# The S5 part in another order, skip and router sums on GpSimd, expert weights in 4 MB pieces

## Chip, cores and metric

The kernel runs on one core of one Trainium2 chip. The metric is the device time of one execution in microseconds (us). A profiled execution comes with it: its span goes from the first to the last instruction, its time also covers what lies around them. Engines are TensorE (PE; weight loads are PEld), VectorE (DVE), ScalarE (ACT), GpSimd (POOL) and SyncE (SP), which issues nearly all transfers.

## What is computed

One layer of a decoder on 256 tokens of width 1024: an S5 state-space mixer (48 groups of 16 channels, 64 complex states each) beside a cross-attention into 256 memory tokens, one output projection, layer norm, a mixture of 32 experts (four for each token), layer norm. All numbers are float32.

```python
p = x @ w_in                                   # 768 columns for S5, 256 for attention
y_mix = s5_mixer(p[:, :768], ...)              # scan over time, + d_skip * u, gelu, y * sigmoid(y @ w_glu + b_glu)
y_mem = attention(p[:, 768:], mem @ w_k, mem @ w_v)       # 4 heads of 64
h = layer_norm(ALPHA * x + concat(y_mix, y_mem) @ w_out, ln1_g, ln1_b)
logits = h @ router_w + router_b               # top 4 of 32, softmax over the four
for e in range(32):                            # only the tokens that chose e
    gu = h @ w_gu[e] + b_gu[e]                 # 1024 -> 2048
    g, l = min(gu[:, :1024], 7), clip(gu[:, 1024:], -7, 7)
    y += gate[e] * ((g * sigmoid(1.702 * g) * (l + 1)) @ w_down[e] + b_down[e])
out = layer_norm(ALPHA * h + y, ln2_g, ln2_b)
```

## The kernel before

**Memory.** One SBUF tile `big` holds 23 slots of 1 MB (128 partitions x 8 KB). `slot_of` gives every named matrix a slot, several names share one in turn. Two neighbouring slots make a block of 2 MB; 11 blocks form `ring`, in the order in which the front part lets go of them. `next_block` turns the ring by one block.

**Order.** Every instruction on TensorE, ScalarE, VectorE and SP is chained to the one before it in the program (`pin`), so each of these engines runs in the order of the text. GpSimd is not chained. A transfer on SP waits until the last reader of its block is done, and all transfers behind it wait too.

**Front part.** S5 runs in 32 chunks of 8 steps. The group matrices `m1p` (state input, three tiles of 16 groups) and `m2` (state output, three tiles) are made by `power` on VectorE, sums partly on GpSimd. `kb` (from line 578) makes the kernels within a chunk, with the skip `dsk` added by a TensorE product with the identity, and ScalarE copies them to `kr`. Then, in the order of the text: first half of K (`kps`), turning of biases and norms (`bgp`, to `gcol` and `bglu`), router bias (`rbp`: `ln1_b @ router_w` on TensorE, 8 products, and one for `router_b`), turning of `kr` (`kc`), copies of it to other rows (`shifted(0)`), second half of K, scores, row maxima, chunk powers (`doubled(NC)`), `shifted(1)`, turning of `m1p` (`m1_turned`, banks `m1tp`), chunk inputs `s_in` (banks `sip`), turning of these (banks `stp`, to `sv`), exponentials, V projection (`vmp`), `shifted(2)`, `rotated` twice (the scan over chunks), reciprocals and products for the softmax, products within the chunk (`yb`, called Yt), attention output (`pTp`, `pv`), `xs` on VectorE, products with the chunk states (`yb`, called Yx), out-projection of the attention, gelu, gate (`zp`), `wsp` (column sums of `router_w * ln1_g`, summed over k by VectorE as `wgs`, then over partitions by TensorE), the rest of the out-projection (`yp`), norm and router.

**Experts.** For each expert SP loads `w_gu` in four pieces of 2 MB, `load_gu` (two k-tiles each; every partition gets 16 KB that lie together in memory), and `w_down` in two. Per expert TensorE does: `up` (banks `gu`, 64 products seen in the trace), for every second expert `gather_pair` (tokens of two experts picked from `h_sb`) or else `combine` (adding two experts' results into `accp`, which the first call also sets up), `act_t` (turning of the activations), `up_bias`, `down`. At the end expert 31's `up` comes ahead of expert 30's `down`; all that uses the banks `tail`. Expert 31's `act_t` stands behind expert 30's `down` and ahead of its own.

Of the kernel before, what the change touches and what calls it, by code (L numbers as in the profile page):

```python
# [28 lines left out]
ROWS = 2  # L29
NBIG = 23  # L30
# [11 lines left out]
def kernel(  # L42
# [47 lines left out]
    )):  # L90
        for name in names.split():
            slot_of[name] = k
# [5 lines left out]

    ring = [2 * k + n for k in (0, 1, 2, 3, 4, 8, 6, 10, 7, 9, 5) for n in range(0, 2, ROWS)]

# [478 lines left out]
    for b in range(3):  # L579
# [41 lines left out]
    dbg("@KM", None)  # L621

    proj("kps", kT, lambda q, kt: wk[:, kt, P * q : P * q + P], lambda q, kt: memT[:, kt, :], (0,))
# [7 lines left out]
    wg, wgs, lfix = keep_t("wg", (P, KT, NE)), small("wgs", (P, NE)), keep_t("lfix", (P, 2, NE))  # L631
# [7 lines left out]
    tv = [t.rearrange("p (g t h) -> p g t h", t=Q, h=NH) for t in tz]  # L639
    for b in range(3):  # L640
        for a in range(2):
            ps = bank(f"kc{b}{a}")
            for l in range(4):
                tr(ps[:, P * l : P * l + P], kr[:, 4 * b + l, NH - NH * a : NH - NH * a + P])
            S.copy(tv[b][:, :, Q - 1 - a, :], ps.rearrange("p (g h) -> p g h", h=2 * NH)[:, :, 0:NH])

    def shifted(b):
        for m, rows in ((1, ((32, 64), (64, 96), (96, 128))), (2, ((64, 128),)), (3, ((96, 128),))):
            for r0, r1 in rows:
                S.copy(  # L650
                    tv[b][r0:r1, :, Q - 2 - 2 * m : Q - 2 * m, :],
                    tv[b][r0 - 32 * m : r1 - 32 * m, :, Q - 2 : Q, :],
                )

    tj = [tz[(g % 12) // 4][:, P * (4 * (g % 4) + g // 12) :][:, 0:P] for g in range(NG)]

    shifted(0)
    dbg("@KM1", None)
    proj("kps", kT, lambda q, kt: wk[:, kt, P * q : P * q + P], lambda q, kt: memT[:, kt, :], (1,))
    dbg("@LG1", None)  # L660
    wgl += load_wgl(1)
    dbg("@SM", None)
    scores = []
    for i in range(2):
        sc = [bank(f"sc{i}{e}") for e in range(2)]
        for h2 in range(2):
            for e in range(2):
                pe = slice(64 * e, 64 * e + 64)
                mm(
                    sc[e][:, NT * h2 : NT * h2 + NT], xqT[pe, h2, i * P : (i + 1) * P], kT[pe, h2, :],  # L670
                    True, True, True,
                )
        scores.append(sc)

    dbg("@SMb", None)
    prob = big_tile("prob").rearrange("p (i h m) -> p i h m", i=2, h=4)
    sums = []
    for i, sc in enumerate(scores):
        mx, sm = small(f"mx{i}", (P, 4)), small(f"sm{i}", (P, 4))
        for e in range(2):  # L680
            V.tensor_reduce(
                out=mx.rearrange("p (h e) -> p e h", e=2)[:, e, :],
                in_=sc[e].rearrange("p (h m) -> p h m", h=2), axis=AX.X, op=ALU.max,
            )
        ts(mx, mx, -0.125, ALU.mult)
        sums.append((mx, sm))
    doubled(NC)
    shifted(1)
# [44 lines left out]
    for i, sc in enumerate(scores):  # L733
        mx, sm = sums[i]
        for hd in range(4):
            S.activation(
                prob[:, i, hd, :], sc[hd % 2][:, NT * (hd // 2) : NT * (hd // 2) + NT], AF.Exp,
                bias=mx[:, hd : hd + 1], scale=0.125, accum_out=sm[:, hd : hd + 1],
            )
    dbg("@VM", None)  # L740
    proj("vmp", vm, lambda q, kt: memT[:, kt, P * q : P * q + P], lambda q, kt: wv[:, kt, :], (0,))
    shifted(2)
    dbg("@VM1", None)
    proj("vmp", vm, lambda q, kt: memT[:, kt, P * q : P * q + P], lambda q, kt: wv[:, kt, :], (1,))

    dbg("@SC1", None)
# [7 lines left out]
    def rotated(o, x0, x1, op):  # L754
# [3 lines left out]
        V.tensor_tensor_scan(out=o, data0=r8f, data1=ta, initial=0.0, op0=ALU.mult, op1=ALU.add)  # L758

    rotated(g_re, s_re, s_im, ALU.add)  # L760
    dbg("@SMr", None)
    for i, (_, sm) in enumerate(sums):
        V.reciprocal(sm, sm)
        for hd in range(4):
# [693 lines left out]
```

## Time and profile before

| | us |
|---|---|
| median of three runs | 1074.6 (1073.11 to 1078.62) |
| the profiled execution, its time | 1072.42 |
| its span | 1070.6 |
| TensorE busy | 1003.3 (94% of the span) |
| VectorE / ScalarE / GpSimd busy | 245.6 / 150.4 / 49.2 |

The DMA engines read 421.9 MB from HBM, 402.7 MB of it expert weights. The page's chain of work that ended last gives 50% of the span to TensorE and 45% to DMA. Matmuls are pipelined and their ends are modelled, so a busy TensorE isn't one at its peak.

### The profile page before, as it was taken

How to read it: one execution, taken by the hardware profiler on the slowest of the kernel's cores; microseconds unless marked ns; L12 is line 12 of the kernel's file. 1: busy time of each engine (PE TensorE's matmuls, PEld its weight loads, DVE VectorE, ACT ScalarE, POOL GpSimd, SP SyncE). 2: the span in 40 equal slices, each digit the busy share in tenths (PEclk: the TensorE clock that was granted, in tenths of full speed). 3: DMA queues.
4: the chain of work that ended last, by engine and by line, in shares of the span. 5: the costliest groups of instructions: out<-in, count | busy, mean ns of one | idle time of the engine just before them, and what ended most of it. 6: DMA issues, size and time to landing. Idle time of an engine off the chain costs nothing.

```text
span 1070.6 us, 12357 instructions
## 1 busy us (share of the span) xinstructions
PE 1003.3 (94%) x5297; PEld 442.6 (41%) x5297; DVE 245.6 (23%) x531; ACT 150.4 (14%) x288; POOL 49.2 (5%) x90
## 2 busy tenths in 40 slices
PE   9999999999999999999999988899999999898994
PEld 8886554434343434343434332323333343333331
DVE  7984251111111111111111111110111111111113
ACT  3494020101010101010101000000101110100001
POOL 5810000000000000000000000000000000000001
PEclk9999999999999999999999999999999999999998
DMA  9949989999999999999999999999999999999992
GB/s 303 166 151 329 424 314 429 428 417 430 427 428 427 425 429 428 426 430 427 428 426 429 429 409 428 429 428 427 427 427 428 427 428 427 427 428 428 429 422 98
DMA packets 43939, 424.61 MB, mean 397 GB/s; under 512 B 11251, under 2 KB 14215, under 8 KB 19177
## 3 DMA queue, kind: packets, MB, share of 16 engines
q1 hardware_dynamic: 43384, 422.73, 95.9%
q10 hardware_dynamic: 496, 1.05, 0.3%
q8 instruction: 43, 0.70, 0.3%
q14 instruction: 16, 0.12, 0.0%
HBM read 421.93 MB, written 1.84 MB: 396 GB/s over the span
## 4 chain that ended last, share of the span: by engine, by line
PE 50%; DMA 45%; DVE 2%; ACT 1%; issue 0%; SPq 0%; ACTq 0%; POOL 0%; DVEq 0%; POOLq 0%
DMA big<-in_exp_w_gu_dram 29%; PE gu_e L142 20%; PE dn_e L142 11%; DMA big<-in_exp_w_down_dram 11%; PE xgp_e L142 4%; DMA big<-in_exp_b_down_dram 4%; PE accp L142 3%; PE yp L142 3%; DVE big L135 2%; PE ups L142 1%; PE zp L142 1%; DMA big<-in_l_w_in_dram 1%; PE tail L142 1%; ACT big L135 1%; PE atp_e L145 1%; PE qps L142 1%
## 5 line engine op out<-in xcount | busy, mean ns | idle before, releaser
L142 PE MATMUL gu_e<-big,xg_e 128*64 128x512 f32 x1984 | 439.8, 594 | 44.2 <-DMA big<-in_exp_w_gu_dram 43.5
L142 PEld LDWEIGHTS gu_e<-big,xg_e 128*64 128x64 f32 x1984 | 138.3, 137 | 340.0 <-issue 253.0
L142 PE MATMUL dn_e<-big,xl_te 128*64 128x512 f32 x960 | 212.6, 595 | 0.0
L142 PEld LDWEIGHTS dn_e<-big,xl_te 128*64 128x64 f32 x960 | 66.3, 137 | 144.3 <-issue 119.6
L1127 DVE TENSOR_SCALAR xl_e<-gu_e 128x512 f32<-128x512 f32 x31 | 21.4, 691 | 429.2 <-PE gu_e L142 429.2
L1155 DVE COPY y_e<-dn_e 64x512 f32<-64x512 f32 x30 | 20.5, 684 | 265.7 <-PE dn_e L142 265.7
L135 ACT ACTIVATE gu_e<-xl_e 128x512 f32<-128x512 f32 x31 | 18.6, 601 | 403.7 <-DVE xl_e L1127 403.7
L142 PEld LDWEIGHTS xgp_e<-oh_e,big 128*128 128x128 f32 x544 | 65.4, 196 | 13.3 <-PE gu_e L142 12.2
L142 PE MATMUL xgp_e<-oh_e,big 128*128 128x128 f32 (+1 forms) x544 | 68.7, 284 | 0.0
L142 PE MATMUL accp<-y_e,ogT_e 128*128 128x512 f32 x128 | 59.4, 603 | 0.8 <-DVE y_e L1155 0.8
L135 ACT COPY y_e<-dn_e 64x512 f32<-64x512 f32 x30 | 17.5, 582 | 244.0 <-DVE y_e L1155 244.0
L142 PEld LDWEIGHTS accp<-y_e,ogT_e 128*128 128x128 f32 x128 | 23.2, 190 | 35.3 <-issue 33.7
L142 PE MATMUL gu_e<-bgu,ident 32*64 32x512 f32 x248 | 34.3, 612 | 0.0
L135 DVE TENSOR_TENSOR big<-big 128x96 f32<-128x96 f32 (+8 forms) x47 | 29.0, 635 | 21.1 <-ACT big L135 16.2
L142 PE MATMUL yp<-big 128*128 128x512 f32 x64 | 28.6, 596 | 0.0
L135 DVE TENSOR_TENSOR big<-big,tab 128x2048 f32<-128x2048 f32 x12 | 26.5, 2276 | 0.2 <-DVE big L135 0.2
L135 ACT COPY xl_te<-atp_e 128x512 f32<-128x512 f32 x30 | 17.9, 595 | 60.4 <-PE atp_e L145 57.5
L135 ACT COPY xg_e<-xgp_e 128x512 f32<-128x512 f32 x32 | 18.8, 587 | 53.4 <-PE xgp_e L142 53.4
L1131 DVE TENSOR_TENSOR xr_e<-xr_e,gu_e 128x512 f32<-128x512 f32 x31 | 21.3, 687 | 6.4 <-ACT gu_e L135 3.3
L135 POOL TENSOR_TENSOR yv<-yv,mhalf 128x1 f32<-128x1 f32 x2 | 1.1, 550 | 468.9 <-DVE yv L135 468.9
L1238 POOL MEMSET big<- 128x1280 f32 (+1 forms) x2 | 2.1, 1058 | 447.0 <-PE gu_e L142 447.0
L1130 DVE SCALAR_TENSOR_TENSOR xr_e<-xr_e,xl_e 128x512 f32<-128x512 f32 x32 | 22.1, 692 | 1.1
(289 smaller groups left out, 586.7 us busy)
## 6 DMA issues: line engine op xcount, KB each, us to landing
big<-in_exp_w_gu_dram SPq DMA_DIRECT2D x128, 2048.0 KB, 39.1
big<-in_exp_w_down_dram SPq DMA_DIRECT2D x62, 2048.0 KB, 33.8
big<-in_l_w_in_dram SPq DMA_DIRECT2D x3, 1024.0 KB
big<-in_w_out_dram SPq DMA_DIRECT2D x3, 1024.0 KB, 9.2
big<-in_exp_w_down_dram SPq DMA_DIRECT2D x3, 1024.0 KB
big<-in_x_dram SPq DMA_DIRECT2D x3, 512.0 KB, 3.5
big<-in_l_s_w_glu_dram SPq DMA_DIRECT2D x2, 768.0 KB
big<-in_l_w_in_dram SPq DMA_DIRECT2D x2, 512.0 KB, 6.8
```

What stands on the lines that cost most here:

```text
L135: return lambda *a, **k: pin(f(*a, **k))
L142: pin(PE.matmul(o, lhsT, rhs, start=start, stop=stop, skip_group_check=shared))
L145: pin(PE.transpose(o, in_, ident if idn is None else idn))
L1127: V.tensor_scalar(out=xl_, in0=ps[0], scalar1=7.0, scalar2=None, op0=ALU.min)
L1130: V.scalar_tensor_tensor(out=xr, in0=xr, scalar=1.0, in1=xl_, op0=ALU.add, op1=ALU.mult)
L1131: a = V.tensor_tensor(out=xr, in0=xr, in1=sg, op=ALU.mult)
L1155: eng(y[:, 512 * dh : 512 * dh + 512], ps[dh][64 * dh : 64 * dh + 64, :])
L1238: G.memset(t[:, 0:width], 0.0)
```

## The change

- In the text, `m1_turned` (three tiles), `s_in` and `sv` move up to right behind `bgp`, ahead of `kc`. The first half of K moves behind `kc`. `shifted(1)`, `doubled(NC)` and the first `rotated` come ahead of the row maxima, as does the first half of V with `shifted(2)`; the second `rotated` comes ahead of the reciprocals.
- The skip is added by GpSimd to `kr` instead of by TensorE in the bank. For the router bias GpSimd multiplies `router_w * ln1_b`, VectorE sums it over k, and `wsp` sums both over partitions and adds `router_b`; `rbp` is gone.
- Slots are renumbered so that the ring is 0, 2, 4 to 20 and blocks that follow each other in it mostly lie side by side; `s_in` shares another slot.
- `w_gu` is cut in groups of four k-tiles (a partition has 32 KB that lie together). For experts 3 to 28, where the two blocks are neighbours, one transfer of 4 MB takes both; otherwise two of 2 MB. The gather follows the new numbering.
- Expert 31's `act_t` comes between the two halves of expert 30's `down`.

```diff
@@ ring and slots
+    free_order = (0, 1, 2, 3, 4, 8, 6, 10, 7, 9, 5)
-        "ptmp0 wsc", "ptmp1 gt", "m20", "m21", "m22", "u_sb", "cab s_in tw yg", "memT xs", "bbt tz0", "bab att",
-        "mem_sb tz1 gb", "ut kr pT x2", "x_sb m1p1 wgl2", "xT prob", "rawb m1p2 wo0", "rawc m1p0 wo1", "win_2 wo3",
+        "ptmp0 wsc", "ptmp1 gt", "m20", "m21", "m22", "u_sb", "cab tw yg", "memT xs", "bbt tz0", "bab att",
+        "mem_sb tz1 gb", "ut kr pT x2", "x_sb m1p1 wgl2", "xT s_in prob", "rawb m1p2 wo0", "rawc m1p0 wo1", "win_2 wo3",
-            slot_of[name] = k
+            slot_of[name] = 2 * free_order.index(k // 2) + k % 2 if k < 22 else k
-    ring = [2 * k + n for k in (0, 1, 2, 3, 4, 8, 6, 10, 7, 9, 5) for n in range(0, 2, ROWS)]
+    ring = list(range(0, 22, ROWS))
@@ kb
-        mm(pv_[:, :, 0:NH], ident, dsk[:, 4 * b : 4 * b + 4, :], False, True, True)
         S.copy(kr[:, 4 * b : 4 * b + 4, NH:144], pv_)
+    tt(kr[:, :, NH : 2 * NH], kr[:, :, NH : 2 * NH], dsk, ALU.add, G)
@@ behind doubled(16)
-    proj("kps", kT, lambda q, kt: wk[:, kt, P * q : P * q + P], lambda q, kt: memT[:, kt, :], (0,))
...
     S.copy(bglu, bgp[:, 0:6])
-    rbp = bank("rbp")
-    for kt in range(KT):
-        mm(rbp[:, 0:NE], gcol[:, KT + kt : KT + kt + 1].to_broadcast([P, P]), wr[:, kt, :], kt == 0, False)
-    mm(rbp[:, 0:NE], ones[0:1, :], rb, False, True)
-    S.copy(lfix[:, 1], rbp[:, 0:NE])
+    def m1_turned(j):
...
+    m1t = m1_turned(0)
+    m1t += m1_turned(1)
+    m1t += m1_turned(2)
+    s_in = big_tile("s_in")[:, 0:1536].rearrange("p (l n) -> p l n", l=6)
...
@@ behind kc
+    proj("kps", kT, lambda q, kt: wk[:, kt, P * q : P * q + P], lambda q, kt: memT[:, kt, :], (0,))
     shifted(0)
@@ behind the scores
+    shifted(1)
+    doubled(NC)
...
+    rotated(g_re, s_re, s_im, ALU.add)
+    proj("vmp", vm, lambda q, kt: memT[:, kt, P * q : P * q + P], lambda q, kt: wv[:, kt, :], (0,))
+    shifted(2)
@@ behind the second half of V
-    rotated(g_re, s_re, s_im, ALU.add)
+    rotated(g_im, s_im, s_re, ALU.subtract)
     for i, (_, sm) in enumerate(sums):
         V.reciprocal(sm, sm)
...
-    rotated(g_im, s_im, s_re, ALU.subtract)
@@ router
-    tt(wg, wr, gcol[:, 0:KT].unsqueeze(2).to_broadcast([P, KT, NE]), ALU.mult, G)
+    for q, w_ in enumerate((wg, wb)):
+        tt(w_, wr, gcol[:, KT * q : KT * q + KT].unsqueeze(2).to_broadcast([P, KT, NE]), ALU.mult, G)
...
-    V.tensor_reduce(out=wgs, in_=wg.rearrange("p k e -> p e k"), axis=AX.X, op=ALU.add)
+    for q, w_ in enumerate((wg, wb)):
+        V.tensor_reduce(out=wgs[:, q], in_=w_.rearrange("p k e -> p e k"), axis=AX.X, op=ALU.add)
...
-    mm(wsp[:, 0:NE], ones, wgs, True, True)
+    mm(wsp[:, 0 : 2 * NE], ones, wgs.rearrange("p q e -> p (q e)"), True, False)
+    mm(wsp[:, NE : 2 * NE], ones[0:1, :], rb, False, True)
     S.mul(lfix[:, 0], wsp[:, 0:NE], -1.0)
+    S.copy(lfix[:, 1], wsp[:, NE : 2 * NE])
@@ gather
-    hv = h_sb.rearrange("p i (t r j) -> p i t j r", r=P, j=ROWS)
+    hv = h_sb.rearrange("p i (t r j) -> p i t j r", r=P, j=GJ)
@@ down
+            if kk == KT // 2:
+                between()
@@ load_gu
+        for t in range(KT // GJ):
+            rows = src[t * GJ * P : (t + 1) * GJ * P, :].rearrange("(p j) n -> p j n", j=GJ)
+            next_block(), next_block()
+            k0, k1 = ring[-2:]
+            if whole and k1 == k0 + ROWS:
+                b = big[:, 2048 * k0 : 2048 * (k0 + GJ)].rearrange("p (j n) -> p j n", j=GJ)
+                SP.dma_start(b, rows)
+                w += [b[:, j, :] for j in range(GJ)]
+                continue
+            for n, k in enumerate((k0, k1)):
+                b = big[:, 2048 * k : 2048 * (k + ROWS)].rearrange("p (j n) -> p j n", j=ROWS)
+                SP.dma_start(b, rows[:, ROWS * n : ROWS * n + ROWS])
+                w += [b[:, j, :] for j in range(ROWS)]
@@ the experts' loop
+        gu = load_gu(w_gu[0, e], 3 <= e < NE - 3) if e < NE - 1 else gu_last
...
-            down(f"e{e}", at, lambda kk: dn[kk], y[0:64, :], [tb[0]] * 2)
+            last_at = []
+            down(
+                f"e{e}", at, lambda kk: dn[kk], y[0:64, :], [tb[0]] * 2,
+                lambda: last_at.append(act_t(f"e{e + 1}", a, tb[3])),
+            )
...
-            at = act_t(f"e{e}", a, tb[3])
-            down(f"e{e}", at, lambda kk: dn[kk], y[64:P, :], tb[1:3])
+            down(f"e{e}", last_at[0], lambda kk: dn[kk], y[64:P, :], tb[1:3])
```

## Rows read from the trace of the kernel before

**Rows 1.** The page: slices of transfer rate (26.8 us each); a DMA issue line.

```profile
GB/s 303 166 151 329 424 314 429 428 417 430 427 428 427 425 429 428 426 430 427 428 426 429 429 409 428 429 428 427 427 427 428 427 428 427 427 428 428 429 422 98
...
big<-in_exp_w_gu_dram SPq DMA_DIRECT2D x128, 2048.0 KB, 39.1
```

**Rows 2.** Windows: us, then busy us (instructions) by engine, PEclk, DMA share, GB/s.

```profile
134.00:140.00 6.00, 6.00 (x33) 4.04 (x32) 4.62 (x13) 0.59 (x1) 0.00 (x0) 1.00 0.24 55
...
240.00:1040.00 800.00, 755.16 (x3662) 290.67 (x3660) 120.81 (x252) 71.30 (x132) 2.05 (x2) 1.00 1.01 427
```

**Rows 3.** Timeline, TensorE at the end: start us, us, engine, line, instruction [idle before].

```profile
1042.06 3.65 PE L142 MATMUL tail<-big 128*64 128x512 f32 x16 [1.14 <-DMA big<-in_exp_w_down_dram]
...
1045.64 0.75 PE L145 MATMUL tail<-ident,xr_e 128*128 128x128 f32 x4
...
1047.72 7.09 PE L142 MATMUL tail<-big,xl_te 128*64 128x512 f32 x32 [1.33 <-ACT xl_te L135]
```

**Rows 4.** Timeline of VectorE in the front part.

```profile
62.20 1.27 DVE L135 TENSOR_REDUCE mx<-sc 128x2 f32<-128x512 f32 x2
...
64.98 1.95 DVE L135 TENSOR_TENSOR big<-big,e__413 128x384 f32<-128x384 f32 x4
...
72.02 2.88 DVE L135 TENSOR_TENSOR big<-big 128x768 f32<-128x768 f32 x3 [4.15 <-PE stp L145]
74.93 1.76 DVE L135 TENSOR_TENSOR_SCAN big<-big 128x768 f32<-128x768 f32 x1
...
81.37 7.48 DVE L135 TENSOR_TENSOR big<-big 128x744 f32<-128x744 f32 x8
```

**Rows 5.** Timeline of ScalarE in the front part.

```profile
55.90 3.13 ACT L135 COPY big<-big 32x512 f32<-32x512 f32 x5
...
62.61 5.97 ACT L135 COPY big<-m1tp 128x512 f32<-128x512 f32 x12
...
71.09 1.83 ACT L135 COPY big<-stp 128x512 f32<-128x512 f32 x4
...
76.41 0.43 ACT L135 COPY big<-vmp 128x256 f32<-128x256 f32 x1
```

**Rows 6.** Timeline of TensorE in the front part.

```profile
43.16 0.43 PE L142 MATMUL kb<-dsk,ident 128*128 128x64 f32 x2
...
46.19 3.67 PE L142 MATMUL kps<-big 128*128 128x256 f32 x16
...
52.63 2.84 PE L145 MATMUL kc<-ident,big 128*128 128x128 f32 x24
...
58.86 2.19 PE L142 MATMUL sc<-big 64*128 64x256 f32 x16
...
72.07 7.07 PE L142 MATMUL vmp<-big 128*128 128x256 f32 x32
```

**Rows 7.** A window of 2 us behind the stream.

```profile
1050.00:1052.00 2.00, 2.00 (x12) 0.64 (x10) 0.00 (x0) 0.00 (x0) 0.00 (x0) 1.00 0.08 33
```

**Rows 8.** Timeline of SP's queue: single issues of expert 4's blocks.

```profile
216.63 0.33 SPq L135 DMA_DIRECT2D big<-in_exp_w_gu_dram  x1
...
232.98 0.33 SPq L135 DMA_DIRECT2D big<-in_exp_w_gu_dram  x1
```

**Rows 9.** A window of 1 us after that issue.

```profile
234.00:235.00 1.00, 1.00 (x8) 0.37 (x6) 0.00 (x0) 0.00 (x0) 0.00 (x0) 1.00 1.16 328
```

**Rows 10.** DMA packets from 300 to 360, 1044 to 1052 and 16 to 20 us.

```profile
DMA packets 1763, 25.65 MB, mean 427 GB/s; under 512 B 197, under 2 KB 197, under 8 KB 197
...
q1 hardware_dynamic: 1760, 25.61, 100.4%
...
DMA packets 314, 1.48 MB, mean 185 GB/s; under 512 B 43, under 2 KB 43, under 8 KB 223
...
q1 hardware_dynamic: 314, 1.48, 45.0%
...
q1 hardware_dynamic: 375, 1.46, 98.0%
```

More of the change, by code (lines that the diff above doesn't have):

```diff
@@ L29 @@
 ROWS = 2
+GJ = 4
 NBIG = 23
@@ L630 @@
     S.copy(bglu, bgp[:, 0:6])
-    wg, wgs, lfix = keep_t("wg", (P, KT, NE)), small("wgs", (P, NE)), keep_t("lfix", (P, 2, NE))
-    rbp = bank("rbp")
-    for kt in range(KT):
-        mm(rbp[:, 0:NE], gcol[:, KT + kt : KT + kt + 1].to_broadcast([P, P]), wr[:, kt, :], kt == 0, False)
-    mm(rbp[:, 0:NE], ones[0:1, :], rb, False, True)
-    S.copy(lfix[:, 1], rbp[:, 0:NE])
[L639 to L687, printed above, removed]
@@ L688 @@
-    shifted(1)
+    wg, wb = keep_t("wg", (P, KT, NE)), small("wb", (P, KT, NE))
+    wgs, lfix = small("wgs", (P, 2, NE)), keep_t("lfix", (P, 2, NE))
     dbg("@M1B", None)
@@ L731, with shifted @@
             S.copy(dst[:, l0:l1], ps[:, 0 : P * (l1 - l0)].rearrange("p (l j c) -> p l j c", j=4, c=NC))
[L733 to L744, printed above, removed]
+    tv = [t.rearrange("p (g t h) -> p g t h", t=Q, h=NH) for t in tz]
+    for b in range(3):
+        for a in range(2):
+            ps = bank(f"kc{b}{a}")
+            for l in range(4):
+                tr(ps[:, P * l : P * l + P], kr[:, 4 * b + l, NH - NH * a : NH - NH * a + P])
+            S.copy(tv[b][:, :, Q - 1 - a, :], ps.rearrange("p (g h) -> p g h", h=2 * NH)[:, :, 0:NH])
+    def shifted(b):
+        for m, rows in ((1, ((32, 64), (64, 96), (96, 128))), (2, ((64, 128),)), (3, ((96, 128),))):
+            for r0, r1 in rows:
+                S.copy(
+                    tv[b][r0:r1, :, Q - 2 - 2 * m : Q - 2 * m, :],
+                    tv[b][r0 - 32 * m : r1 - 32 * m, :, Q - 2 : Q, :],
+                )
+    tj = [tz[(g % 12) // 4][:, P * (4 * (g % 4) + g // 12) :][:, 0:P] for g in range(NG)]
+    dbg("@KM", None)
+    proj("kps", kT, lambda q, kt: wk[:, kt, P * q : P * q + P], lambda q, kt: memT[:, kt, :], (0,))
+    shifted(0)
+    dbg("@KM1", None)
+    proj("kps", kT, lambda q, kt: wk[:, kt, P * q : P * q + P], lambda q, kt: memT[:, kt, :], (1,))
+    dbg("@LG1", None)
+    wgl += load_wgl(1)
+    dbg("@SM", None)
+    scores = []
+    for i in range(2):
+        sc = [bank(f"sc{i}{e}") for e in range(2)]
+        for h2 in range(2):
+            for e in range(2):
+                pe = slice(64 * e, 64 * e + 64)
+                mm(
+                    sc[e][:, NT * h2 : NT * h2 + NT], xqT[pe, h2, i * P : (i + 1) * P], kT[pe, h2, :],
+                    True, True, True,
+                )
+        scores.append(sc)
+    shifted(1)
+    doubled(NC)
     dbg("@SC1", None)
@@ L760 @@
     rotated(g_re, s_re, s_im, ALU.add)
+    dbg("@VM", None)
+    proj("vmp", vm, lambda q, kt: memT[:, kt, P * q : P * q + P], lambda q, kt: wv[:, kt, :], (0,))
+    shifted(2)
+    dbg("@SMb", None)
+    prob = big_tile("prob").rearrange("p (i h m) -> p i h m", i=2, h=4)
+    sums = []
+    for i, sc in enumerate(scores):
+        mx, sm = small(f"mx{i}", (P, 4)), small(f"sm{i}", (P, 4))
+        for e in range(2):
+            V.tensor_reduce(
+                out=mx.rearrange("p (h e) -> p e h", e=2)[:, e, :],
+                in_=sc[e].rearrange("p (h m) -> p h m", h=2), axis=AX.X, op=ALU.max,
+            )
+        ts(mx, mx, -0.125, ALU.mult)
+        sums.append((mx, sm))
+    for i, sc in enumerate(scores):
+        mx, sm = sums[i]
+        for hd in range(4):
+            S.activation(
+                prob[:, i, hd, :], sc[hd % 2][:, NT * (hd // 2) : NT * (hd // 2) + NT], AF.Exp,
+                bias=mx[:, hd : hd + 1], scale=0.125, accum_out=sm[:, hd : hd + 1],
+            )
+    dbg("@VM1", None)
+    proj("vmp", vm, lambda q, kt: memT[:, kt, P * q : P * q + P], lambda q, kt: wv[:, kt, :], (1,))
+    rotated(g_im, s_im, s_re, ALU.subtract)
     dbg("@SMr", None)
@@ L1143, in act_t, with down @@
         return at
-    def down(n, at, w_of, y, ps=None):
+    def down(n, at, w_of, y, ps=None, between=lambda: None):
         ps = [bank(f"dn_{n}")] * 2 if ps is None else ps
         for kk in range(KT):
+            if kk == KT // 2:
+                between()
             w = w_of(kk)
@@ L1181, in combine_on, with load_gu @@
                 tt(acc[:, i, ds_], acc[:, i, ds_], ps, ALU.add)
-    def load_gu(src):
+    def load_gu(src, whole=False):
         w = []
-        for t in range(KT // ROWS):
-            b = next_block().rearrange("p (j n) -> p j n", j=ROWS)
-            SP.dma_start(b, src[t * ROWS * P : (t + 1) * ROWS * P, :].rearrange("(p j) n -> p j n", j=ROWS))
-            w += [b[:, j, :] for j in range(ROWS)]
+        for t in range(KT // GJ):
[11 more added lines that the diff above has]
+                w += [b[:, j, :] for j in range(ROWS)]
         return w
```

7 lines of the change are left out of this document (3 added, 4 removed).

## The prediction

> **What bounds the kernel now.** Read first the page's slices of transfer rate [rows 1]: from the sixth slice on (each is 26.8 us) the core's DMA engines move about 428 GB/s to the end, while the six slices before that are uneven. The windows [rows 2] say the same sharply: 427 GB/s at a share of 1.01 from 240 to 1040 us, and 55 GB/s from 134 to 140. So all sixteen engines work without a pause from 140 us on, and the weights of 32 experts (32 x 12.58 MB) pass through them in order. Eight of the ring's 2 MB blocks come free and are loaded before 134 us; the rest, some 386 MB, starts when the output projection lets go of the next blocks at about 140 us, and 386 MB at 427.5 GB/s is 903 us, which gives 1043 us. The trace has TensorE taking up the last block but those of the last expert at 1042.06 [rows 3]. Three things therefore set the time: when the front part hands over (140 us), how long the stream runs (903 us), and what comes behind it (28.5 us up to 1070.6). In the stream TensorE first works off its lead of eight blocks and then waits for weights; time saved on it there is worth nothing. The times below go by the profiled execution, 1072.4 us with a span of 1070.6; the median of the three runs is 1074.6, 2.2 above it, and I add that at the end.
>
> **The front part.** Up to 89 us VectorE, ScalarE and TensorE hand each other work. In the trace of before VectorE idles 4.15 us ahead of the first rotation, waiting for the turned chunk states `stp` [rows 4], since ScalarE copies the twelve banks of `m1tp` only from 62.6 to 68.6 [rows 5]. The change puts this block ahead of `kc`, the K projection and the scores. I follow the new chain with the old durations.
> TensorE leaves `kb` at 46.2 [rows 6]; the three products with `dsk` (0.43 each) are gone, so at 45.0. ScalarE has copied `kb`, `gcol` and `bglu` at about 46, then the twelve `m1tp` copies take 5.97: 52.0. From there to the last `stp` copy it was 4.3 us before (68.6 to 72.9) [rows 5]: 56.3. VectorE is in its own queue until 62.2, then `doubled(NC)` takes 3.0 and the first rotation 4.8 [rows 4]: 70.0. So the old wait is gone, and what is late next is the other branch. TensorE: `kc` after `stp`, 2.84, until 58.7; first K projection 3.67 until 62.4. ScalarE copies it (0.43 for such a copy of `vmp` [rows 5]) and then, behind it in its queue, runs `shifted(0)` (3.13) until 65.9; the second projection is done at 66.1 and copied at 66.5; of the scores (2.19) the last three quarters need both halves of K: 68.1. V projection, first half of 7.07: 71.6; copy and `shifted(2)` on ScalarE: 75.1; the eight exponentials, which lay between `stp` and the copy of `vmp`, take 3.6 [rows 5]: 78.7. VectorE has been done with the row maxima (2.8) at 72.8 and with the second rotation (4.6) at 77.4, but now **the reciprocals stand ahead of the products for `xs` in its queue** and wait for the exponentials: `xs` starts at 79.0 and takes 7.48 [rows 4], so it ends at 86.5, and the Yx products on TensorE start there instead of at 88.85. That is 2.4 us. Behind it TensorE is busy without a break up to the end of the output projection, and one product is added ahead of the latter: the router bias joins `wsp`, and a small product of two instructions lasts about 0.4, as those with `dsk` do [rows 6], some 0.3 of it on the path. GpSimd's two router products and VectorE's second sum over them lie beside TensorE's products with `w_glu`; with that cover gone the second sum, of 256 elements a row, would cost less than a product of 768 does, 0.96 (2.88 for three [rows 4]). So the hand-over comes **2.1 us earlier**. The best case is VectorE never waiting: 62.2 + 3.0 + 4.8 + 2.8 + 4.6 + 7.5 = 84.9, 4.0 earlier. The worst is nothing: GpSimd makes the `kr` sum, which no row shows, and if it is queued behind the second `m2` sum, TensorE and all that follows may start some 2 us later.
> All SP issues of this part keep their order; the copy of `x2` waits for `pv` as before, and the idle stretch at 134 to 140 us swallows small delays of the eight blocks ahead of it.
>
> **The tail.** Before, TensorE turned the last expert's activations after the last product of expert 30: products of the second half from 1042.06, turning at 1045.64, ScalarE's copy behind another copy, and the last expert's products only at 1047.72 [rows 3]. Now the turning stands between the two halves, where TensorE waits 1.14 us for weights anyway (four turnings, 0.75), and the copy is hidden behind the second half. The last products start at 1045.64: **2.1 us** less. They need their weights: the engines are nearly done at 1050 (share 0.08 from there to 1052 [rows 7]), and the last two k-tiles are wanted at 1051 and 1051.9, so they just arrive in time; were they late, 1.1 us would be lost. Bounds: 1.0 to 2.1 saved.
>
> **The 4 MB pieces, cost.** A whole piece takes two neighbouring blocks of the ring, so SP waits for the later one. Over most of the stream there is enough in flight (39 us from issue to landing in the median [rows 1]) for that to cost nothing. Early on there isn't. For expert 4 SP issued its third 2 MB block at 216.63 and the fourth at 232.98 [rows 8], since no block comes free while TensorE builds `accp` and then starts expert 2's second product. Around 234 to 235 the rate falls to 328 GB/s [rows 9]: the queue was just running dry when the fourth arrived. After the change the third is tied to the fourth and goes out at 233 with it. The queue is then 2 MB poorer when it counts: 2.1 MB at 427.5 GB/s is **4.9 us** of idle engines, and since the stream is the bound it is never made up. Behind SP's wait stand only loads whose blocks come free later still. The same happens once before, at expert 3, whose third block is tied to a fourth that comes free later, but whatever idles there shortens the later queue no further: together one block. Further on what is in flight grows from expert to expert, up to the 39 us [rows 1], and no gap as long as this 16 us comes again, since `accp` is set up only once: I count no other dry spot. Bounds: 3.9 (the engines that lag were not dry yet) to 5.7.
>
> **The 4 MB pieces, gain.** Each partition's run grows from 16 to 32 KB, half as many packets. In a window of nothing but expert weights [rows 10] 1566 data packets of 16 KB take 100.4% of 16 x 60 us: 614 ns each. Near the end 91 packets of 8 KB and 180 of 4 KB (1.48 MB) take 45.0% of 16 x 8 us, 57 us. With a constant c per packet and one rate both hold for c = 9 ns. Per 4 MB piece each engine saves eight constants and one small closing packet, which I price at the constant too: 9 x 9 = 81 ns. By the ring (11 blocks, 10 from expert 18 on) 44 pairs of experts 3 to 28 are neighbours, 41 of them behind the dry spot: 41 x 81 ns = **3.3 us** saved. Bounds: 0, if 32 KB still moves as two packets of 16, since the trace has none above 16; and 8.5, by the early window of 4 KB packets [rows 10], where 98.0% of 64 us over 375 packets is 167 ns for 3.9 KB, so c = 23 ns. I take 9, from the same kind of load.
> The Trainium skill speaks of both ends. Its page "DMA: Bandwidth & Descriptors", section "Rules for kernel authors", asks for 128 partitions and at least 1 MiB per DMA for full bandwidth; the 2 MB pieces satisfy that, so by it the gain would be 0. The same page, "Why small descriptors are slow (HBM only)", names about three fixed cycles per packet; at the 850 MHz that it gives for the fabric that is by my estimate 3.5 ns, less than the 9 ns of the rows, and the gain would be 1.3 us. The rows decide for 9 ns.
>
> **Other edits.** The gather reads `h_sb` with a stride of four elements instead of two; the turning of activations reads with a stride of four already, and TensorE has slack in the stream: nothing. The renumbered ring keeps its order: nothing.
>
> **Sum.** 1072.4 - 2.1 - 2.1 + 4.9 - 3.3 = 1069.8; on the scale of the median, **1072.0**.
>
> **The rivals.** (a) 32 KB moves as two packets of 16: the gain falls away, 1072.0 + 3.3 = 1075.3. For it: no packet above 16 KB in the trace. Chance 0.20. (b) The dry spot does not cost: the queue holds more than I read, or the lagging engines ride through it, 1072.0 - 4.9 = 1067.1. Against it: the 328 GB/s at 234. Chance 0.20. (c) A packet costs 23 ns beyond its bytes, 1072.0 - 5.2 = 1066.8. Chance 0.10. (d) **Slower**: a 32 KB packet takes longer than two of 16. Two take 1228 ns; with 41 pieces of eight packets on each engine every 15 ns above that is 4.9 us, and from rival (a)'s 1075.3 that is 1080.2; it decides for slower from about 1243 ns. Against it: time is linear from 4 to 16 KB [rows 10]. Chance 0.05. The skill's page on DMA has in "Latency and other measured facts" copies that lose rate at large power-of-two row pitches; the pitch here doubles to 32 KB, and no row here shows such a loss.
>
> **How the numbers follow.** The forecast has 0.45, its own range 1069 to 1075. A measurement of this kernel tells about 0.5% from no change, 5.4 us: below 1069.2 is faster, above 1080.0 slower. Cases (b) and (c) are faster, (d) slower, the forecast and (a) the same: faster 0.30, same 0.65, slower 0.05. For 8 in 10 I take 1066 (between (b) with a good front and (c)) to 1077 ((a) with the front worth nothing).
>
> **What would show it.** Right: Yx starts near 86.5, VectorE's wait ahead of the first rotation is gone and one ahead of a reciprocal is there; the transfer rate has a hole of some 5 us at 225 to 235; the rate from 300 to 360 us is about 429; the last products follow the ones before without a gap. Wrong: no hole, packets of 16 KB as before, or TensorE rather than the stream deciding the middle.

## The result, and the profile after

| | before | after |
|---|---|---|
| median, us | 1074.56 (1073.11 to 1078.62, 4 runs) | 1085.74 (1084.16 to 1086.46, 4 runs) |
| profiled execution: time, span | 1072.42, 1070.6 | 1084.16, 1082.5 |
| TensorE busy in the span | 1003.3 (94%) | 1059.4 (98%) |

The ratio is 1.0108 [1.0087, 1.0129]: the change makes the kernel 1.1% slower. The forecast was 1072.0 with 1066 to 1077, so the time lies outside the range. In short: the longer transfers raise the rate a little, as they were meant to, but the new layout makes the gather read its weights at a wider stride, those loads take much longer, and early in the run TensorE then lets go of blocks too late, so that the stream of weights falls behind and never makes it up.

The page of after: the engines' busy time, then (from the second part) the granted clock, which is the TensorE clock that the throttle allowed (in tenths of the full 2.4 GHz; 9 is 90% or more), and the transfer rate in 40 slices of 27.1 us, then the chain that ended last.

```profile
PE 1059.4 (98%) x5275; PEld 510.2 (47%) x5275; DVE 247.6 (23%) x532; ACT 150.4 (14%) x288; POOL 50.4 (5%) x92
...
PEclk9999988999999999999999999999999999999998
...
GB/s 301 161 180 308 411 261 345 347 428 388 434 423 428 430 430 432 434 427 429 430 430 430 430 415 419 429 431 429 437 427 428 428 427 434 421 429 427 428 424 138
...
PE 92%; DMA 4%; DVE 2%; ACT 1%; SPq 0%; issue 0%; ACTq 0%; POOL 0%; DVEq 0%; POOLq 0%
```

The chain that was half TensorE and half DMA is now TensorE for 92% of the span, and the transfer rate, which stood at its level from the seventh slice on [rows 1], is weaker in the sixth (261) and now also in the seventh, eighth and tenth (345, 347 and 388). What grew is seen in the groups of instructions, first of before, then of after (busy us, mean ns of one | idle before, releaser):

```profile
L142 PE MATMUL gu_e<-big,xg_e 128*64 128x512 f32 x1984 | 439.8, 594 | 44.2 <-DMA big<-in_exp_w_gu_dram 43.5
...
L142 PEld LDWEIGHTS xgp_e<-oh_e,big 128*128 128x128 f32 x544 | 65.4, 196 | 13.3 <-PE gu_e L142 12.2
L142 PE MATMUL xgp_e<-oh_e,big 128*128 128x128 f32 (+1 forms) x544 | 68.7, 284 | 0.0
```

```profile
L144 PE MATMUL gu_e<-big,xg_e 128*64 128x512 f32 x1984 | 434.6, 596 | 2.9 <-DMA big<-in_exp_w_gu_dram 2.2
...
L144 PEld LDWEIGHTS xgp_e<-oh_e,big 128*128 128x128 f32 x544 | 128.3, 329 | 13.0 <-PE gu_e L144 12.2
L144 PE MATMUL xgp_e<-oh_e,big 128*128 128x128 f32 (+1 forms) x544 | 131.5, 402 | 0.0
```

One form nearly doubled: the gather (`xgp`), whose stationary operand is `h_sb` at the new stride. A load takes 329 ns where it took 196, and on the chain of work that ended last the gather of a pair of experts takes 7.66 us where it took 3.97. TensorE's waits for `w_gu` fell from 43.5 to 2.2 us. In sum TensorE is busy 56.1 us longer, and its idle time (span less busy) shrank by 44.2 us, from 67.3 to 23.1; the difference is the 11.9 us that the span grew.

Where the stream lost its lead: windows of before (first fence) and of after (us, busy us by engine, granted clock as a share of full, busy share of the DMA engines, GB/s).

```profile
136.00:300.00 164.00, 160.58 (x807) 68.40 (x808) 34.17 (x90) 16.92 (x31) 0.55 (x1) 0.99 0.98 413
...
150.00:160.00 10.00, 10.00 (x48) 3.31 (x46) 2.31 (x9) 2.82 (x6) 0.00 (x0) 1.00 0.98 372
170.00:180.00 10.00, 10.00 (x48) 3.31 (x46) 0.68 (x1) 0.58 (x1) 0.00 (x0) 1.00 0.99 421
```

```profile
136.00:300.00 164.00, 160.62 (x726) 77.79 (x727) 33.50 (x89) 16.36 (x30) 0.55 (x1) 0.95 0.89 369
...
150.00:160.00 10.00, 9.27 (x36) 4.59 (x38) 2.71 (x11) 3.64 (x7) 0.00 (x0) 0.65 0.65 226
170.00:180.00 10.00, 10.00 (x44) 8.06 (x46) 2.07 (x6) 1.17 (x2) 0.00 (x0) 0.70 1.00 428
...
300.00:900.00 600.00, 600.00 (x2754) 263.07 (x2752) 90.36 (x193) 54.50 (x101) 2.05 (x2) 1.00 1.00 428
```

Up to 300 us the DMA engines stand still for (0.98 - 0.89) x 164 = 14.8 us more: TensorE frees the blocks of the first experts later. From 300 on TensorE and the stream are both full, and the rate is no lower than the 427 GB/s of before [rows 2]: the loss is made ahead of 300 us.

The first experts on TensorE, before and after the change (start us, us):

```profile
144.11 2.10 PE L142 MATMUL xgp_e<-oh_e,big 128*128 128x64 f32 x16
...
149.80 13.95 PE L142 MATMUL gu_e<-big,xg_e 128*64 128x512 f32 x64 [0.73 <-ACT xg_e L135]
...
163.89 3.98 PE L142 MATMUL xgp_e<-oh_e,big 128*128 128x64 f32 x32
```

```profile
143.80 4.00 PE L144 MATMUL xgp_e<-oh_e,big 128*128 128x64 f32 x16
...
148.98 3.81 PE L144 MATMUL xgp_e<-oh_e,big 128*128 128x64 f32 x16
153.52 15.64 PE L144 MATMUL gu_e<-big,xg_e 128*64 128x512 f32 x64 [0.73 <-ACT xg_e L137]
...
169.31 7.73 PE L144 MATMUL xgp_e<-oh_e,big 128*128 128x64 f32 x32
```

Beside the gathers the first expert's products are longer, 15.64 us where before they took 13.95: the granted clock stood at half, 1.2 GHz, in part of this stretch (0.65 and 0.70 in the two windows above, where before had 1.00 in both). It fell between 146 and 148 us, where the mean is 0.68, amid the first slow gathers.

### The profile page after: what moved, and what is told of

The parts are those of the page before. It is cut to its first block, busy times and chain, and to the rows that moved or that the text cites. A ratio compares the mean times of both kernels' runs of the same rounds, so it can differ in the third digit from the quotient of the medians.

```text
span 1082.5 us, 12213 instructions
## 1 busy us (share of the span) xinstructions
PE 1059.4 (98%) x5275; PEld 510.2 (47%) x5275; DVE 247.6 (23%) x532; ACT 150.4 (14%) x288; POOL 50.4 (5%) x92
## 3 DMA queue, kind: packets, MB, share of 16 engines
q1 hardware_dynamic: 37048, 422.73, 94.4%
## 4 chain that ended last, share of the span: by engine, by line
PE 92%; DMA 4%; DVE 2%; ACT 1%; SPq 0%; issue 0%; ACTq 0%; POOL 0%; DVEq 0%; POOLq 0%
PE gu_e L144 41%; PE dn_e L144 19%; PE xgp_e L144 12%; PE accp L144 5%; DMA big<-in_exp_w_gu_dram 3%; PE tail L144 3%; PE yp L144 3%; PE ups L144 2%; PE zp L144 1%; PE atp_e L147 1%; ACT big L137 1%; DVE big L137 1%; DMA big<-ud 1%; PE kps L144 1%; PE busy L144 1%; DMA ud<-big 0%
## 5 line engine op out<-in xcount | busy, mean ns | idle before, releaser
L144 PE MATMUL gu_e<-big,xg_e 128*64 128x512 f32 x1984 | 434.6, 596 | 2.9 <-DMA big<-in_exp_w_gu_dram 2.2
L144 PEld LDWEIGHTS gu_e<-big,xg_e 128*64 128x64 f32 x1984 | 142.9, 138 | 288.9 <-issue 284.6
L144 PEld LDWEIGHTS xgp_e<-oh_e,big 128*128 128x128 f32 x544 | 128.3, 329 | 13.0 <-PE gu_e L144 12.2
L144 PE MATMUL xgp_e<-oh_e,big 128*128 128x128 f32 (+1 forms) x544 | 131.5, 402 | 0.0
L153 DVE TENSOR_SCALAR oh_e<-iota,rk 128x64 f32<-128x64 f32 x62 | 12.8, 252 | 85.2 <-PE xgp_e L144 85.2
```

The costliest lines, as they stand in the source:

```text
L144: pin(PE.matmul(o, lhsT, rhs, start=start, stop=stop, skip_group_check=shared))
L153: return (eng or V).tensor_scalar(out=o, in0=x0, scalar1=s1, scalar2=s2, op0=op0, op1=op1)
```

## The experiments

Three theories stood against each other. S: the stride of the gather alone makes the loss. P: the 4 MB pieces make it (the dry spot, or 32 KB packets that are slow). F: the front part's new order makes it. All ratios are to the kernel before, run on the same chip.

**The stride alone.** The kernel before, with

```diff
-    hv = h_sb.rearrange("p i (t r j) -> p i t j r", r=P, j=ROWS)
+    hv = h_sb.rearrange("p i (t r j) -> p i t j r", r=P, j=4)
```

> The kernel before with one change: the gather reads its weights out of h_sb at a stride of four elements instead of two (it picks other columns, so its result is another; everything else is as before). Theory S (the stride makes weight loads slow and TensorE the bound): the loads of xgp take about 330 ns instead of 196, a pair gather 7.7 us instead of 4.0, TensorE hardly waits for weights, and the time is about 1085 us (1082 to 1089). Rival P (the 4 MB pieces hold TensorE up): 1074.6, as before. Rival F (the front part's order is at fault): 1074.6.

Measured: 1086.77 us (ratio 1.012 [1.0072, 1.0167]):

```profile
L142 PE MATMUL gu_e<-big,xg_e 128*64 128x512 f32 x1984 | 432.9, 594 | 2.2 <-DMA big<-in_exp_w_gu_dram 1.4
...
L142 PEld LDWEIGHTS xgp_e<-oh_e,big 128*128 128x128 f32 x544 | 128.3, 329 | 13.3 <-PE gu_e L142 12.2
```

S holds: this line alone costs what the whole change costs. It costs it early. From 136 to 300 us this kernel moves 377 GB/s where before moved 413, which puts it 5.9 MB or 13.8 us behind, and its span is 13.9 us longer; from 300 to 900 both move 427.

**Everything but the stride.** The changed kernel with `j=2` in that line; other columns of `h` are gathered by it.

> The changed kernel with one change: the gather reads h_sb at a stride of two again, while the weights come in groups of four k-tiles (it picks other columns, so its result is another). Theory S: pair gathers 4.0 us, transfers are the bound again, and the rest of my sum can be seen: front 0.8 earlier as its trace shows, tail 2.1, hole 4.9, packets 3.3: 1073 us, 1069 to 1076. Rival P or F: it stays near 1085.7.

Measured: 1071.84 us (ratio 0.9984 [0.9958, 1.0009]); by the medians the stride of the changed kernel is worth 13.9 us, by the two ratios 13.3. The rest of the change gives 2.3 us by the medians (by the interval 4.5 less to 1.0 more); the sum had 2.6. Three of its steps can be read here. The windows around the dry spot (the hole in the transfer rate that the prediction called so) and in the stream, and TensorE at the end:

```profile
220.00:230.00 10.00, 10.00 (x42) 3.97 (x42) 0.00 (x0) 0.59 (x1) 0.00 (x0) 1.00 0.88 375
230.00:240.00 10.00, 10.00 (x50) 3.41 (x48) 0.68 (x1) 0.58 (x1) 0.00 (x0) 1.00 0.91 364
...
300.00:900.00 600.00, 573.66 (x2756) 224.49 (x2758) 92.15 (x196) 54.81 (x103) 2.05 (x2) 0.98 1.01 429
...
1039.56 3.65 PE L144 MATMUL tail<-big 128*64 128x512 f32 x16 [0.49 <-DMA big<-in_exp_w_down_dram]
1043.04 3.60 PE L144 MATMUL tail<-big,xl_te 128*64 128x512 f32 x16
1046.95 3.65 PE L144 MATMUL tail<-big,xl_te 128*64 128x512 f32 x16 [0.31 <-DMA big<-in_exp_w_down_dram]
```

The hole is there, about 2.1 us of idle engines in these two windows (0.12 and 0.09 of 10 us). In the stream the DMA queue shows fewer packets and more bytes, before and then this kernel, 300 to 900 us:

```profile
DMA packets 17623, 256.06 MB, mean 427 GB/s; under 512 B 1967, under 2 KB 1967, under 8 KB 2001
```

```profile
DMA packets 12779, 257.30 MB, mean 429 GB/s; under 512 B 1430, under 2 KB 1430, under 8 KB 1464
```

**How the load's time goes with the stride.** The kernel before with `j=8`, and with three elements (`h_sb[:, i, a : a + 382 : 3]`); other columns are read.

> The kernel before with the gather's reading of h_sb at a stride of eight elements; which columns are read is changed by it, and nothing else. Theory (the weight load of a 128x128 tile costs more the further apart its elements lie, from four on): the LDWEIGHTS of the gather, 196 ns at a stride of two and 330 at four, takes about 600 ns, a pair's gather 14 to 15 us, and the kernel about 1200 us. Rival (two levels only, neighbours within a small distance or not): 330 ns as at four, and 1087 us. Rival (strides of four and eight read the same banks of something, eight worse than linear): over 700 ns.

> The kernel before with the gather's weights read at a stride of three elements (twelve bytes); which columns are read is changed by it, and nothing else. So far the load of a 128x128 tile took 192 ns for neighbours, 196 at a stride of two, 330 at four and 335 at eight: two levels. Theory (the second level begins at four elements, sixteen bytes): 196 ns, a pair's gather 4.0 us, and the kernel at 1072 to 1075 us. Rival (it begins at three): 330 ns, 7.7 us, 1086 us. Rival (a level between): some 260 ns, and 1074 to 1080 us.

> The gather at a stride of three elements once more, since its one time, 1085.5 us, is as long as at four although its pair of gathers takes 5.80 us and not 7.66. Theory (from 300 us on a pair of experts still costs TensorE 55.6 + 1.8 = 57.4 us against 58.9 of the stream, so only the experts up to 250 us, whose gathers delay the blocks that come free, cost time, and that run's front part began 2 us late and met a low clock): a median of 1074 to 1080 us. Rival (every added microsecond of gather counts, also where TensorE has slack): 1084 to 1088 us.

The gather's loads at 8 and at 3, the latter of the second run (min/median/max ns):

```profile
L142 PEld LDWEIGHTS xgp_e<-oh_e,big x544: 312/335/338, 144.5 to 1009.3; 128*128 128x128 f32 x182
```

```profile
L142 PEld LDWEIGHTS xgp_e<-oh_e,big x544: 251/262/333, 147.0 to 1001.9; 128*128 128x128 f32 x182
```

| stride, float32 elements | 1 | 2 | 3 | 4 | 8 |
|---|---|---|---|---|---|
| median of a load, ns | 192 | 196 | 262 | 330 | 335 |
| gather of a pair, us | | 3.97 | 5.80 | 7.66 | |
| time, us | | 1072 to 1075 | 1084.98 | 1086.77 | 1086.37 (one run) |

The first run at three had the same median of a load and 1085.51 us (one run). Both expectations missed in their first theory: 600 ns at a stride of eight, and 196 at three, where the load came out as in the last rival (260) and the time as in the one before it (1086). There are neither two levels nor a steady rise: flat up to two, halfway at three, flat again from four. What fits all five rows is the number of elements that lie in one piece of 16 bytes: 4, 2, 1.33, 1 and 1; that this is the cause was not tested any other way. The Trainium skill, page "SBUF — State Buffer", section "Door 1: The DMA port swizzle", has this as a rule: SBUF is read in lines of 16 bytes, and full speed needs at least two accesses in a line. The five medians agree with that; where its next sentence calls strides of up to four float32 free, they bear out two.

The time at a stride of three fell outside what I expected (1074 to 1080) and on the number of its rival, 1084.98 (ratio 1.0101 [1.0063, 1.0139]). The rival's reason isn't borne out: from 300 to 900 us TensorE is busy 588.81 of 600, over the run it still waits 20.7 us for `w_gu`, and the rate is 427. The loss is made early (385 GB/s from 136 to 300), with half clock in part of it, and in this run's trace the front part was late too (first gather at 147.0, before 144.1):

```profile
150.00:160.00 10.00, 9.27 (x38) 6.46 (x39) 3.65 (x15) 3.64 (x7) 0.00 (x0) 0.53 0.77 295
180.00:190.00 10.00, 10.00 (x50) 3.36 (x48) 0.68 (x1) 0.58 (x1) 0.00 (x0) 1.00 0.80 306
...
300.00:900.00 600.00, 588.81 (x2784) 243.45 (x2782) 91.05 (x194) 55.10 (x102) 2.05 (x2) 1.00 1.01 427
```

I had counted the gathers up to 250 us and no change of the clock. Between 145 and 181 us it fell to half in every trace with slow loads, and in none of before and of `a_stride2`; in the turned kernels below it falls in some too, so slow loads aren't its only cause. How much of the early loss is clock and how much gather isn't separated by any run; the turned kernel with whole pieces from expert 6, whose loads are fast, had 0.59 and 0.56 from 140 to 160 us and moved 395 GB/s from 136 to 300, so a part of it can be the clock's alone.

**The stride taken away, the pieces kept.** `h_sb` is stored turned, so that the gather reads neighbours, and in a second kernel all pieces are 2 MB:

```diff
+    hv = h_sb.rearrange("p i (t j r) -> p i t j r", r=P, j=GJ)
+    hq = hv.rearrange("p i t j r -> p i t r j")
-        stt(h_sb[:, i, hs], h_sb[:, i, hs], rs[i], gb[:, 1, hs], ALU.mult, ALU.add)
+        stt(hq[:, i, hf], hq[:, i, hf], rs[i], split(gb[:, 1, hs]), ALU.mult, ALU.add)
...
-                    mm(accp[i][hf], alpha_id, h_sb[:, i, 512 * hf : 512 * hf + 512], True, False)
+                    mm(accp[i][hf].rearrange("p (r j) -> p r j", j=GJ), alpha_id, hq[:, i, hf], True, False)
```

> The changed kernel with h_sb stored turned by VectorE's norm (k-tiles of 128 columns lie together), so that the gather's weights are contiguous; the start of accp reads it at a stride instead. Theory S: loads of xgp about 190 ns, 1073 us as with stride two, up to 2 us more if VectorE's strided writes are slower. Rival P or F: near 1085.7.

> As the kernel with h_sb stored turned, and every piece of w_gu 2 MB (whole pieces off). By my sum for the pieces (hole 4.9, packets 3.3) it is 1.6 us faster than that one. If 4 MB pieces save packets and cost no hole it is 3.3 us slower; if they cost the hole and save nothing 4.9 us faster.

Measured: 1077.74 us (ratio 1.0023 [0.9999, 1.0048]) and 1075.02 (1.0011 [0.9984, 1.0038]). The loads are back at 192 ns, and the 1085.7 of P and F is out; the first still missed its 1073 to 1075, and by the medians both lie above the kernel that gathers other columns. The two medians lie 2.7 us apart, which the scatter of ten runs each doesn't tell from the forecast's 1.6; that the second be 3.3 us slower is out. A cost of storing turned shows on two engines: the products that set up `accp` read their moving operand at a stride of 128 and take 1050 ns instead of 592 at full clock, and VectorE's norm takes 1.11 instead of 0.74 us. That these make up the gap isn't shown: the first kernel's trace also has a clock of 0.52 from 150 to 160 us.

**Whole pieces only from expert 6 on.**

```diff
-        gu = load_gu(w_gu[0, e], 3 <= e < NE - 3) if e < NE - 1 else gu_last
+        gu = load_gu(w_gu[0, e], 6 <= e < NE - 3) if e < NE - 1 else gu_last
```

> The changed kernel with h_sb stored turned, so that the gather reads neighbouring elements, and with whole 4 MB pieces only from expert 6 on. Theory dry spot (tying the third block of expert 4 to its fourth runs the queue dry once, about 5 us, and 4 MB pieces otherwise gain about 0.5% of the stream): no hole in the transfer rate at 225 to 245 us, some 3 to 5 us less than the same kernel with whole pieces from expert 3 on (1077.7), that is 1073 to 1075. Rival (the hole costs nothing, because another stretch sets the time): the same 1077 to 1078. Rival (whole pieces gain nothing): as with all pieces of 2 MB, 1075, with 427 GB/s from 300 to 900 us and not 429.

Measured: 1069.84 us (ratio 0.9964 [0.9943, 0.9984]), by the ratios 0.6% better than with whole pieces from expert 3: some 6 us, more than the 3 to 5 that were expected. No early expert waits for a neighbouring block now, and the engines are full up to 240 us. A small hole is left, behind the slow `accp`:

```profile
230.00:240.00 10.00, 10.00 (x37) 3.71 (x37) 0.00 (x0) 0.59 (x1) 0.00 (x0) 0.97 1.00 426
240.00:250.00 10.00, 10.00 (x48) 3.30 (x46) 0.68 (x1) 0.58 (x1) 0.00 (x0) 1.00 0.85 339
```

**The tail alone, and the front with the tail.** The kernel before with expert 31's `act_t` between the halves of expert 30's `down`; and the changed kernel without 4 MB pieces and with a stride of two.

> The kernel before with one part of the change, the turning of the last expert's activations between the two halves of expert 30's products. The prediction's step gives -2.1 us against the kernel before (ratio 0.998), with the last products taken up right behind the ones before them. Rival (their weights are not there yet): -1.0. Rival (the end is set by the last transfer and not by TensorE): 0, with a wait for the last down weights of some 2 us in the last products.

> The changed kernel without its third part: pieces of w_gu of 2 MB and the gather at a stride of two elements, as before; the front's new order, the GpSimd sums, the renumbered ring and the tail stay. By the prediction's steps -4.2 us against the kernel before (2.1 front, 2.1 tail), ratio 0.996. By the trace of the changed kernel, where Yx starts 0.8 to 1.4 us earlier and not 2.4, about -3.2. Rival (a dip of the granted clock between 80 and 160 us takes the front's gain back): -2.1 to +2 and a profile whose clock in that stretch is below that of the kernel before.

Measured: 1072.01 us (0.9986 [0.9967, 1.0004]) and 1072.44 (0.9985 [0.9965, 1.0005]), against 1073.63. The tail gives 1.6 us by the medians (by the interval 3.5 less to 0.4 more, so the forecast's 2.1 lies inside and nothing isn't excluded). Its trace is sharper: from the start of expert 30's second half (1043.43) to the last sums into `accp` (1055.26) it takes 11.83 us, where before took 13.52 (1042.06 to 1055.58), 1.7 us less. The front on top of it gives nothing that shows. In the profile of the second, the Yx products that follow `xs` start at 88.44 against 88.91, the experts start no earlier (143.10 against 143.09), and the clock stood at 0.83 from 80 to 90 us where before had 1.00: this fits the rival named ahead of the run, a lower clock that takes the gain back. The same front in `a_stride2`, with 1.00 from 80 to 90, hands over at 141.99, 1.1 us earlier than before.

**ScalarE's queue in the front.** On the front with the tail: the eight exponentials ahead of `shifted(2)`, and the scaled identity for `accp` made early, in the tile `lower` (TensorE waited 2.45 us for it).

```diff
-    shifted(2)
     dbg("@SMb", None)
...
                 bias=mx[:, hd : hd + 1], scale=0.125, accum_out=sm[:, hd : hd + 1],
             )
+    shifted(2)
```

> The changed kernel with pieces of 2 MB and a gather at a stride of two, with two edits of its own: ScalarE runs the eight exponentials ahead of shifted(2) and not behind it, and the scaled identity for accp is made in expert 0 and not behind expert 2's activation. Theory of the front (ScalarE's queue, vmp copy, shifted(2), exponentials, sets when the reciprocals run and with them xs): the reciprocals stand 1.5 to 2.5 us earlier, VectorE's wait of 1.65 us ahead of the second reciprocal is gone, Yx starts 1.5 to 2 us earlier than in the same kernel without the two edits (88.4), and the time is 1.5 to 2 us below its 1072.4, 1070.5. Rival (VectorE's own queue is late next, or a lower granted clock at 80 to 90 us takes it back): the same 1072. TensorE's wait of 2.45 us ahead of accp is gone in either case; the queue is full there, so that alone gives nothing.

Measured: 1070.39 us (0.9966 [0.9949, 0.9983]), the time that was expected, 2 us below the same kernel without the edits; the two intervals overlap. VectorE's wait ahead of the second reciprocal shrank, from 1.65 us to this:

```profile
79.25 0.18 DVE L137 RECIPROCAL sm<-sm 128x4 f32<-128x4 f32 x1 [0.52 <-ACT big L137]
```

TensorE is next: `pv` now ends after `xs`, so that counted from ScalarE's copy of `vmp` Yx comes 0.75 us earlier (14.19 instead of 14.94), not 1.5 to 2. On the clock of the run it even comes later, at 89.39 against 88.44, behind a slower `sip` (4.49 us instead of 2.83) at a granted clock of 0.83 from 50 to 60 us. So the time came out as expected without its mechanism; whether the 2 us are real, and which of the two edits would make them, is open. The second edit did more than end the wait: `accp`'s products take 3.70 us instead of 5.23, with no stretch of half clock among them.

**Both together.** The same two edits on the turned kernel with whole pieces from expert 6; VectorE and the `accp` products go through `h_sb` in its stored order.

```diff
-                    mm(accp[i][hf].rearrange("p (r j) -> p r j", j=GJ), alpha_id, hq[:, i, hf], True, False)
+                    mm(split(accp[i][hf]), lower, hv[:, i, hf], True, False)
```

> The same two edits on the kernel with h_sb stored turned and 4 MB pieces from expert 6 on (1069.8 without them), and two more: VectorE writes h_sb in its stored order and reads its inputs at a stride of four elements instead of writing at a stride of 128, and the products that set up accp read h_sb in its stored order and write PSUM at a stride of four. Theory (a TensorE product that reads its moving operand at a stride of 128 elements, and a VectorE instruction that writes so, run slower: 1050 instead of 592 ns, 1.1 instead of 0.74 us; in the stored order they don't): accp back at 592 ns each, VectorE's instructions back at about 0.7, no dip of the clock at 140 to 160 us, no hole in the rate at 240 to 245 us, and 1069.8 less 1.4 (the hole) less 1.5 to 2 (front), 1066.5 to 1067. Rival (writing PSUM, or reading in VectorE, at a stride of four is as slow): accp stays near 1050 ns, and 1068 to 1069.

Measured: 1067.95 us (ratio 0.9942 [0.9916, 0.9967]), clear of before, and by the medians below both kernels, with intervals that overlap theirs. The `accp` products are back at 592 ns, so writing PSUM at a stride of four costs nothing that the trace shows; of VectorE the rival was right, 1.13 us where it was 1.11 before the edit. First the turned kernel, then this one:

```profile
L144 PE MATMUL accp<-big,xl_alpha x8: 1048/1050/1118, 225.0 to 231.2; 128*128 128x512 f32 x8
```

```profile
L144 PE MATMUL accp<-big,lower x8: 592/592/697, 218.6 to 221.7; 128*128 128x512 f32 x8
```

The dip of the clock at 140 to 160 us did not go (0.83), only the hole at 240 us did.

## Why the prediction was wrong

**The step that failed** is "Other edits": the gather at a stride of four, "the turning of activations reads with a stride of four already, and TensorE has slack in the stream: nothing". Both halves fail.

- That the turning reads at a stride of four was taken for a sign that it is free, and its price was not looked up. The trace of before had it, in the loads of two turnings, first at a stride of four, then of neighbours (min/median/max ns):

```profile
L145 PEld LDWEIGHTS atp_e<-ident,xr_e x120: 195/209/240, 167.6 to 991.2; 128*128 128x128 f32 x120
```

```profile
L145 PEld LDWEIGHTS m1tp<-ident,big x48: 137/140/144, 61.0 to 67.0; 128*128 128x128 f32 x48
```

  The stride costs 69 ns a load there, and the gather makes 544 loads: some 38 us of TensorE's time could have been put into the sum as an estimate. It turned out as 134 ns a load.
- The slack was not put in numbers. [rows 2] give them: TensorE is busy 755.16 of 800 us, 94.4%. A pair of experts is 25.2 MB, 58.9 us of the stream at 427 GB/s, so the slack is 3.3 us for a pair; the gather's 3.7 us more uses it up. From 300 us on that costs nothing that shows, the rate stays at 427 to 428. The loss is made earlier, where there is hardly any slack (TensorE busy 160.58 of 164 us in before): there TensorE's pace sets when blocks come free, as the step on the dry spot says itself. The prediction had that wait for its pieces and left it out for the gather.

With what one line costs by the two experiments, 12 to 14 us, the sum would have been 1084 to 1086. The slower rival (d) looked for the loss in packets, where there is none.

**The other steps**, read where the stride doesn't cover them:

- *The bound*: right for before (but the level starts with the seventh slice, the sixth has 314). The last of the signs that were named, "TensorE rather than the stream deciding the middle", is what the chain shows, 92% TensorE.
- *Pieces, gain*: right. Rival (a) falls: the pages count 37048 packets on the weights' queue `q1` instead of 43384, 6336 fewer, which is 44 pieces x (128 + 16), so 32 KB goes as one packet and its closing packet is saved too. From 300 to 900 us the engines move 257.30 instead of 256.06 MB, 2.9 us' worth, over some 303 packets fewer on each engine: 9.6 ns for a packet, where the step had 9. (c) and (d) fall with it.
- *Pieces, cost*: right in kind and place; its size isn't one number. From 200 to 250 us the kernels with whole pieces move less than their like with 2 MB: `a_stride2` 401 GB/s and `a_front_tail` 425, 2.8 us' worth; after 360 and `b_stride4` 400, 4.7; the turned two 364 and 412, 5.6. The pairs differ in their clocks too. So rival (b) falls. [rows 9] is weaker than it was read: its DMA share is 1.16, and single microseconds around it scatter from 328 to 459 GB/s. That the cost can be avoided is shown by the kernel with whole pieces from expert 6.
- *Tail*: right in kind, 1.7 us by the traces of the tail alone and not 2.1. In `a_stride2` the last products follow without a gap at 1043.04, and their last weights come 0.31 us late, of the 1.1 that the step allowed for; [rows 3] had 1.33 of waiting there.
- *Front*: the wait ahead of the first rotation is gone and one ahead of a reciprocal is there, as forecast, but `xs` ends at 88.07 and not 86.5 (before: 88.85), and the experts' first products start at 142.78 instead of 143.09: 0.3 us earlier, not 2.1. What was missed, in after's rows:

```profile
53.23 2.83 PE L144 MATMUL sip<-big 128*32 128x128 f32 x96 [1.96 <-DMA big<-ud]
...
80.52 0.18 DVE L137 RECIPROCAL sm<-sm 128x4 f32<-128x4 f32 x1 [1.65 <-ACT big L137]
80.61 7.46 DVE L137 TENSOR_TENSOR big<-big 128x744 f32<-128x744 f32 x8
...
87.55 2.64 PE L144 MATMUL yb<-big 128*32 128x128 f32 x76
```

`sip` was moved past the landing of `u_sb`, a transfer that before had been long there; I had followed the engines' queues and not SP's. The 1.96 us pass down TensorE's and ScalarE's queues to the exponentials, and so to the reciprocal and `xs`, which starts 1.6 us later than forecast. GpSimd's added products also push its second `m2` sum from 51.68 to 53.45, where it overlaps VectorE's own sum, 4.23 us long where it was 3.04; since VectorE still waits 1.65 us for ScalarE behind it, that delay didn't set `xs`. The clock fell too, to 0.83 from 80 to 90 us.
- *The sum without the stride*: that `a_stride2` came within 0.3 us of the 2.6 us that the sum takes off is in part luck, since front, tail and hole all came out smaller than their terms.

## What to carry to other kernels

Before a layout is changed for the sake of transfers, list every reader of that layout and price each from a row of the same instruction: here the matrix whose columns follow the pieces is loaded by TensorE 544 times. "There is slack" needs a number for each stage, the slack per step against the added time per step; early in this stream, where the reader's pace frees the buffers, there was hardly any. A loss of this kind is found by undoing one line, and here the matrix could be stored once in the order that those loads read.

## What the runs showed of the hardware

- A float32 weight load of 128x128 took 192, 196, 262, 330 and 335 ns at strides of 1, 2, 3, 4 and 8 elements. A moving operand of 512 elements at a stride of 128 took 1050 ns instead of 592, also in the products that ran at full clock; PSUM written at a stride of four, 592.
- VectorE's 512 elements of the norm took 1.11 us written at a stride of 128 and 1.13 read at a stride of four, 0.74 with neither.
- Runs of 32 KB move as one packet, and the stream gains 0.5% by them.
- Times of one kernel scatter by up to 12 us. Of 20 executions of the kernel before on one chip, the 16 with a mean granted clock of 0.991 or more took 1071.2 to 1074.2 us, the four at 0.987 to 0.989 took 1077.7 to 1079.0. Of the kernel before and the one with the tail alone, whose front parts are the same, Yx started at 88.91 and 91.17; in the later one the `kc` turnings took 4.51 us instead of 2.84, at a clock of 0.91 from 40 to 60 us instead of 1.00.
